# Pairs of convolution projections by seven half-size products, and attention operands ordered by residue modulo 4

## The chip, the cores and the metric

The program runs on 1 core of one Trainium2 chip. The metric is device microseconds (us) of one execution. Before the change three timed runs gave 2191.52, 2192.58 and 2193.35 us: the median is 2192.58 us.

## The reference

One inference step of a four-layer decoder for a prompt of 512 tokens and a sample group of 8 tokens, 520 columns in all, in float32. The layers are an mLSTM, a gated short convolution, a dilated attention and a pooling layer. In outline, for the two that matter here:

```python
def shortconv_mixer(h, w_in, conv_w, w_out, buf):      # w_in 1024 x 8192
    bg, cg, xb, z = jnp.split(h @ w_in, 4, axis=-1)
    cx = cg * xb
    cpad = concatenate([buf, cx], axis=1)
    y = conv_w[0] * cpad[:, 0:T] + conv_w[1] * cpad[:, 1:1+T] + conv_w[2] * cpad[:, 2:2+T]
    return (bg * y * silu(z)) @ w_out, cpad[:, -2:]

def dilated_mixer(h, w_in, w_out, pos, caches):        # three groups, dilation 1, 4, 16
    parts = jnp.split(h @ w_in, 10, axis=-1)           # q, k, v of each group, and z
    for each group: q, k = rope(q), rope(k); softmax(q k^T) over keys at that dilation; times v
    return (merge of the three groups * silu(z)) @ w_out, new keys and values
```

In the groups of dilation 4 and 16 a query sees only keys whose position has the same residue modulo 4, so their prompt attention is four blocks of 128 by 128 for each head.

## The kernel before

All activations lie transposed: a tile has 128 features on the partitions and 520 token columns. A layer is a sequence of projections. One projection (`proj`, L213) makes one output tile of 128 features: it takes eight 128 by 128 slices of one weight tile of 128 x 1024 and multiplies each by an activation tile. Float32 accuracy comes from two parts: a weight is split into `wh` and `wl` (`cast`, L169: ACT rounds at L175, DVE subtracts at L177), an activation into `hi` and `lo`, and `mm6` (L193) issues three products, hi with wh, lo with wh and hi with wl, for each of two column halves of 256 and 264: 48 matmuls a projection. The sums stand in PSUM tiles `ps` (two of them, used in turn) and are read out by DVE or ACT.

Weights are fetched by SP (L165) into three `wf` buffers and split into four pairs of `wh` and `wl`. The order of all weight tiles is the table that `plan` (L39) writes; every call of `weights` (L181) issues the split of the tile three ahead and the fetches of two more. All other work of a layer sits in generators that `tick` advances after every second `mm6`, so that ACT, DVE and POOL work stands between the matmuls in program order; each engine then runs its own instructions in that order.

The convolution layer (`conv`, from L782) makes 16 blocks of four projections: xb, cg, bg and z. A block multiplies xb and cg (L799), forms the three taps (L807 to L813), multiplies by bg (L814) and hands z to `gated`, which multiplies and splits the result (L525 to L530) for the output projection with `w_bo`. Its first blocks read activations that are not yet normalised and are scaled on the way out of PSUM.

The attention layer (`attention`, from L822) makes, for each of 8 heads, nine projections (q, k, v of three groups); `scaled` (L266) reads each out of PSUM in token order. POOL and DVE apply the rotary embedding to 32 of the 128 partitions (L875 to L880). In `attn_head` the groups 1 and 2 take every fourth column, `t[:, r:NP:4]`, as operands of the score matmuls (L925) and of the transposes of v (L936). L622 and L697 are the score matmuls and the transposes of the mLSTM layer, on columns that lie side by side.

Of the kernel before, what the change touches and what calls it, by code (L numbers as in the profile page):

```python
# [14 lines left out]
P = 128  # L15
# [13 lines left out]
DILS = (1, 4, 16)  # L29
NROWS = (128, 128, 64)  # L30
# [7 lines left out]

def plan():  # L39

    out = []

    def end(i, name, halves, begun=False):
        cs = range(2 if halves else 1)
        out.extend((name, j, c) if halves else (name, j) for c in cs for j in range(2) if c or not begun)
        out.extend((name, j, c) if halves else (name, j) for j in range(2, KD) for c in cs)
        for j in range(KD):
            if j % 4 == 0:
                out.append(("w_pe", i, j // 4))
            out.append(("w_pg", i, j))  # L50

    for hd in range(H):
        out.extend(("w_a", j) for j in (hd, 8 + hd, 16 + 2 * hd, 17 + 2 * hd, 32 + 2 * hd, 33 + 2 * hd))
    out.extend(("w_a", 48 + j) for j in range(16))
    end(0, "w_ao", True)
    for j in range(16):
        out.extend(("w_b", 16 * q + j) for q in (2, 1, 0, 3))
    end(1, "w_bo", True)
    for hd in range(H):
        out.extend(("w_c", 8 * q + hd) for q in range(9))  # L60
    out.extend(("w_c", 72 + j) for j in range(H))
    end(2, "w_co", False)
    for g in range(4):
        for n, (u, i) in enumerate(POOLED):
            if g and n == 2:
                out.extend(("w_grp", g - 1, i) for i in range(2))
            out.append(("w_d", 16 * u + 4 * g + i))
    out.extend(("w_do", j, 0) for j in range(2))
    out.extend(("w_grp", 3, i) for i in range(2))
    end(3, "w_do", True, True)  # L70
    return out

# [41 lines left out]
class Net:  # L114
    def __init__(self, ctx, tc, d):
# [5 lines left out]
        self.wp = pool("w", bufs=3)  # L121
# [7 lines left out]
        self.gate, self.finish = Gate(0.5), None  # L129
        self.wkeys, self.wf, self.wc = plan(), {}, {}  # L130
        self.wpos = self.ndma = self.ncast = 0
# [28 lines left out]

    def fetch(self, upto):
        while self.ndma < min(upto, len(self.wkeys)):
            key = self.wkeys[self.ndma]
            wf = self.wp.tile([P, 1024], F32, tag="wf", name=self.nm("wf"))
            self.nc.sync.dma_start(wf, self.d[key[0]][key[1:]])  # L165
            self.wf[self.ndma] = wf
            self.ndma += 1

    def cast(self, upto):  # L169
        nc = self.nc  # L170
        while self.ncast < min(upto, len(self.wkeys)):
            self.fetch(self.ncast + 1)
            wf = self.wf.pop(self.ncast)
            wh = self.wp.tile([P, 1024], F32R, tag="wh", name=self.nm("wh"), bufs=4)
            nc.scalar.activation(wh, wf, AF.Copy)  # L175
            wl = self.wp.tile([P, 1024], F32R, tag="wl", name=self.nm("wl"), bufs=4)
            nc.vector.tensor_sub(wl, wf, wh.bitcast(F32))  # L177
            self.wc[self.ncast] = (wh, wl)
            self.ncast += 1

    def weights(self, *key, ahead=4):  # L181
        i = self.wpos
        assert self.wkeys[i] == key, (self.wkeys[i], key)
        self.wpos += 1
        self.cast(i + ahead)
        self.fetch(i + 2 + ahead)
        return self.wc.pop(i)
# [5 lines left out]
    def mm6(self, ps, w, c, a, start, stop, m=P):  # L193
# [8 lines left out]
        for j in range(2):  # L202
            mm(out[j], wl, a[0][:, PARTS[j]], start=False, stop=stop)  # L203

# [8 lines left out]
    def proj(self, name, *idx, a):  # L213
# [5 lines left out]
        for c in range(0, n, 8):  # L219
            w = self.weights(name, *idx, *([c // 8] if n > 8 else []))  # L220
            for k in range(8):
                self.mm6(ps, w, k * P, a[c + k], c + k == 0, c + k == n - 1)
                if k % 2:
                    self.tick()
        return ps[:, BASE : BASE + T]

    def proj_pair(self, name, a, n):

        ps = self.psum(), self.psum()
        for c in range(0, n, 8):  # L230
            w = []
            for lo, hi in ((0, 7), (7, 8)) if c + 8 == n else ((0, 8),):
                for j in range(2):
                    if not lo:
                        w.append(self.weights(name, j, *([c // 8] if n > 8 else []), ahead=4 - j))
# [7 lines left out]
    def need(self, a, i):  # L243

        while len(a) <= i:
# [38 lines left out]

    def ready(self, ps):
# [14 lines left out]
    def finish_norm(self, hs, g0, wait, idle, pace):  # L300
# [6 lines left out]
        def work():  # L307
# [14 lines left out]
            for _ in range(idle):  # L322
                yield
            new = []
# [18 lines left out]


# [994 lines left out]
```

## Time and profile before

| | |
|---|---|
| median of the three timed runs | 2192.58 us |
| the profiled execution | 2191.75 us, span 2190.0 us |
| busy: PE | 2170.4 us, 99% of the span |
| DVE | 1336.6 us, 61% |
| ACT | 784.0 us, 36% |
| POOL | 226.8 us, 10% |
| DMA | 275.17 MB, mean 126 GB/s |

PE is TensorE's matmuls, PEld its weight loads, DVE VectorE, ACT ScalarE, POOL GpSimd, SP the engine that issues the transfers. A row of a group of instructions names the source line, the engine, the operation, the output and inputs (buffer numbers left out), the shapes and the count, then the busy time, the mean duration in ns and the idle time before them.

### The profile page before, as it was taken

How to read it: one execution, taken by the hardware profiler on the slowest of the kernel's cores; microseconds unless marked ns; L12 is line 12 of the kernel's file. 1: busy time of each engine (PE TensorE's matmuls, PEld its weight loads, DVE VectorE, ACT ScalarE, POOL GpSimd, SP SyncE). 2: the span in 40 equal slices, each digit the busy share in tenths (PEclk: the TensorE clock that was granted, in tenths of full speed). 3: DMA queues.
4: the chain of work that ended last, by engine and by line, in shares of the span. 5: the costliest groups of instructions: out<-in, count | busy, mean ns of one | idle time of the engine just before them, and what ended most of it. 6: DMA issues, size and time to landing. Idle time of an engine off the chain costs nothing.

```text
span 2190.0 us, 42581 instructions
## 1 busy us (share of the span) xinstructions
PE 2170.4 (99%) x17788; PEld 2154.2 (98%) x17788; DVE 1336.6 (61%) x2984; ACT 784.0 (36%) x1286; POOL 226.8 (10%) x338
## 2 busy tenths in 40 slices
PE   9999999999999999999999999999999999999998
PEld 8999999999999999999999999999999999999998
DVE  7677676653575344333467877787777466676434
ACT  6444444432442222222333323333335343222233
POOL 1101110100000000000014232232220000000000
PEclk9999999999999999999999999999999999999999
DMA  4643544333232322233233645554545233323421
GB/s 151 203 163 139 184 168 150 98 97 97 90 97 87 97 89 95 92 105 95 83 103 127 187 168 179 172 181 155 184 161 194 87 106 97 97 88 97 124 88 51
DMA packets 104643, 275.17 MB, mean 126 GB/s; under 512 B 33316, under 2 KB 37668, under 8 KB 102404
## 3 DMA queue, kind: packets, MB, share of 16 engines
q1 hardware_dynamic: 104308, 272.41, 38.3%
q8 instruction: 139, 2.28, 0.4%
q14 instruction: 52, 0.43, 0.1%
q10 hardware_dynamic: 144, 0.06, 0.0%
HBM read 249.61 MB, written 22.82 MB: 124 GB/s over the span
## 4 chain that ended last, share of the span: by engine, by line
PE 91%; DVE 3%; ACT 1%; POOL 1%; issue 0%; DMA 0%; SPq 0%; POOLq 0%; DVEq 0%; ACTq 0%
PE ps L199 27%; PE ps L201 27%; PE ps L203 27%; PE ax L925 1%; PE ax L998 1%; PE ax L201 1%; PE ax L203 1%; PE ax L199 1%; PE ax L969 1%; PE ax L654 1%; PE ax L673 1%; DVE wl L177 1%; DVE a L329 0%; POOL a L877 0%; PE ax L936 0%
## 5 line engine op out<-in xcount | busy, mean ns | idle before, releaser
L199 PE MATMUL ps<-hi,wh 128*128 128x256 f32 (+1 forms) x5280 | 1086.3, 287 | 2.1 <-DVE a L278 1.6
L201 PE MATMUL ps<-lo,wh 128*128 128x256 f32 (+1 forms) x5280 | 1062.9, 283 | 0.1
L203 PE MATMUL ps<-hi,wl 128*128 128x256 f32 (+1 forms) x5280 | 1063.1, 283 | 0.0
L199 PEld LDWEIGHTS ps<-hi,wh 128*128 128x128 f32 x5280 | 822.3, 189 | 7.6 <-issue 2.5
L201 PEld LDWEIGHTS ps<-lo,wh 128*128 128x128 f32 x5280 | 819.3, 188 | 0.3 <-DVE lo L530 0.3
L203 PEld LDWEIGHTS ps<-hi,wl 128*128 128x128 f32 x5280 | 818.3, 188 | 0.0
L177 DVE TENSOR_TENSOR wl<-wf,wh 128x1024 fp32r<-128x1024 f32 x344 | 429.2, 1249 | 397.1 <-ACT wh L175 395.5
L175 ACT ACTIVATE wh<-wf 128x1024 fp32r<-128x1024 f32 x344 | 361.0, 1051 | 253.2 <-issue 201.7
L271 ACT ACTIVATE a<-ps 128x520 f32<-128x520 f32 x94 | 56.3, 599 | 247.7 <-PE ps L203 243.5
L876 POOL TENSOR_TENSOR a<-a,a 32x520 f32<-32x520 f32 x48 | 74.0, 1542 | 386.2 <-DVE a L278 199.6
L359 DVE TENSOR_TENSOR x<-ps,x 128x520 f32<-128x520 f32 x32 | 22.4, 699 | 103.4 <-PE ps L203 103.3
L278 DVE TENSOR_TENSOR a<-ps,a 128x520 f32<-128x520 f32 x95 | 65.9, 694 | 25.9 <-PE ps L203 22.5
L282 ACT ACTIVATE a<-a 128x520 f32<-128x520 f32 x43 | 27.5, 639 | 150.2 <-DVE a L278 150.0
L259 ACT ACTIVATE hi<-x 128x520 fp32r<-128x520 f32 x32 | 20.5, 639 | 164.6 <-DVE x L359 164.6
L877 POOL TENSOR_TENSOR a<-a,a 32x520 f32<-32x520 f32 x48 | 66.4, 1384 | 124.8 <-DVE a L875 88.7
L902 ACT ACTIVATE S<-S,nmx 128x128 f32<-128x128 f32 (+1 forms) x96 | 40.0, 417 | 76.1 <-DVE nmx L899 76.1
L252 DVE CUSTOM_DVE_ANT_0 kc<-kc,qb 128x128 f32<-128x128 f32 (+1 forms) x192 | 56.8, 350 | 12.5 <-DMA kc<-kc 12.5
L252 DVE CUSTOM_DVE_ANT_0 vc<-vc,pb 128x128 f32<-128x128 f32 (+1 forms) x192 | 61.6, 379 | 0.0
L880 DVE TENSOR_TENSOR a<-a,a 32x520 f32<-32x520 f32 x48 | 37.2, 776 | 17.3 <-POOL a L877 17.3
L260 DVE TENSOR_TENSOR lo<-a,hi 128x520 fp32r<-128x520 f32 x40 | 28.0, 699 | 31.3 <-ACT hi L259 31.3
L732 DVE SCALAR_TENSOR_TENSOR Ci<-kqb,wv,Ci 128x128 f32<-128x128 f32 x128 | 37.1, 346 | 12.2 <-DMA kqb<-scr_kq 10.1
L528 ACT ACTIVATE hi<-a 128x520 fp32r<-128x520 f32 x40 | 25.4, 635 | 50.6 <-DVE a L525 50.6
(272 smaller groups left out, 1759.7 us busy)
## 6 DMA issues: line engine op xcount, KB each, us to landing
wf<-w_c SPq DMA_DIRECT2D x80, 512.0 KB
wf<-w_a SPq DMA_DIRECT2D x64, 512.0 KB
wf<-w_b SPq DMA_DIRECT2D x64, 512.0 KB
wf<-w_pg SPq DMA_DIRECT2D x32, 512.0 KB
wf<-w_d SPq DMA_DIRECT2D x32, 512.0 KB
pb<-scr_p SPq DMA_DIRECT2D x8, 1292.0 KB
Ci<-C_in SPq DMA_DIRECT2D x16, 512.0 KB
kqb<-scr_kq SPq DMA_DIRECT2D x8, 1024.0 KB
```

Of the source, the lines that this page charges most:

```text
L175: nc.scalar.activation(wh, wf, AF.Copy)
L177: nc.vector.tensor_sub(wl, wf, wh.bitcast(F32))
L199: mm(out[j], wh, a[0][:, PARTS[j]], start=start, stop=False)
L201: mm(out[j], wh, a[1][:, PARTS[j]], start=False, stop=False)
L203: mm(out[j], wl, a[0][:, PARTS[j]], start=False, stop=stop)
L252: self.nc.vector.tensor_tensor_reduce(junk, a, b, 1.0, 0.0, ALU.mult, ALU.add, out)
L271: nc.scalar.activation(dst[:, :T], ps, func, scale=scale)
L278: nc.vector.tensor_mul(dst[:, :T], ps, self.r)
L876: nc.gpsimd.tensor_mul(b[:32], t[:32], cs[0])
L877: nc.gpsimd.tensor_mul(a[:32], a[:32], cs[1])
L880: nc.vector.tensor_add(t[:32], a[:32], b[:32])
L902: nc.scalar.activation(blk, blk, AF.Exp, bias=nmx[:, i : i + 1], scale=SCALE, accum_out=l[:, i : i + 1])
```

## The change

Two parts. **Convolution:** of the 16 blocks the first three stay as they were (`NPLAIN`). In the 13 others the projections xb and cg are made together by `seven`; in the even ones of these (six blocks) bg and z too, in the odd ones (seven blocks) these two stay single. That is 19 pairs. `seven` splits a pair into a 2 x 2 scheme: two weight tiles, two halves of the 1024 inputs (four slices each) and two halves of 260 columns, and makes the four quarter results from seven products instead of eight. A product is 4 slices x 3 parts = 12 matmuls of 260 columns. The sums of weights that this needs are formed on POOL (`sum`), then split like weights into half-size tiles `hs` and `ls`; the sums of activations are formed once, after the norm, in `summed`, and kept. The quarter results are put together on ACT and DVE. The last product of a pair is issued in the middle of what follows (`flush`). The outputs of the convolution are split for `w_bo` only behind the last block, and the first half of the output projection of features 0 and 1 runs slice by slice beside that (`look`). For the single tiles of `w_b` and all of `w_bo`, and for the first tile of a pair, the low part is no longer a DVE subtraction: ACT writes minus wh, and a transfer issued by POOL adds the weight from memory to it (L258 to L260). All weights have a table of times (`due`), by which fetches, splits and sums are placed in program order; `wf` has four buffers.

**Attention:** q, k and v of groups 1 and 2 are written out of PSUM in order of residues, so that the 130 columns of a residue (128 prompt, 2 sample) lie side by side; a second pair of rotary tables in that order is loaded; the host puts the keys and values back in order.

```diff
+RES = T // 4
...
+NPLAIN = 3
+HALF = T // 2
+FBUFS, HBUFS, SBUFS = 4, 4, 4
+MOVED = ("w_b", "w_bo")
...
+def paired(j):
+
+    return 0 if j < NPLAIN else 2 - j % 2
...
+            one = at(max(ld, ld2, t - 12.8), i, "sum")
+            h1 = at(max(ld, take("wh", t + 5.76), t - 14.4), i, "high")
...
+        def low(k, tag, n=1024, pool=None):
+            t["l" + k] = new(tag, n, pool)
+            if k == "1" and it.moved:
+                nc.scalar.activation(t["l1"], f(t["h1"]), AF.Copy, scale=-1.0)
+                key = it.keys[0]
+                nc.gpsimd.dma_start(t["l1"], self.d[key[0]][key[1:]], accum_op=ALU.add)
+                return
+            nc.vector.tensor_sub(t["l" + k], t["w" + k], f(t["h" + k]))
...
+            nc.gpsimd.tensor_add(s1, w2[:, a], w2[:, b])
+            sub(w2[:, a], w1[:, a], w2[:, a])
+            sub(s2, s1, w1[:, a])
+            sub(s4, w1[:, b], s2)
...
+    def seven(self, keys, B, dst, done):
...
+        def product(out, w, name, start):
+            for k in range(4):
+                c = slice(k * P, (k + 1) * P)
+                hi, lo = B[name][k]
...
+                mm(out, w[0][:, c], hi, start=start and k == 0, stop=False, **go)
+                mm(out, w[0][:, c], lo, start=False, stop=False, **go)
+                mm(out, w[1][:, c], hi, start=False, stop=k == 3, **go)
...
+        def last():
+            product(r5, part("s4"), "22", False)
+            add(dst[0][:, HALF:], r5, u2)
+            done()
+            step()
+
+        product(r1, part("1", a), "11", True)
+        nc.scalar.activation(s1, r1, AF.Copy)
+        step()
+        product(r6, part("s2"), "T2", True)
+        add(u2, r6, s1)
+        step()
+        product(r5, part("s1"), "T1", True)
+        step()
+        product(r1, part("1", b), "21", False)
+        nc.scalar.activation(dst[0][:, :HALF], r1, AF.Copy)
+        step()
+        self.flush()
+        product(r6, part("2", a), "T3", False)
+        add(u3, r6, s1)
+        step()
+        product(r4, part("2", b), "T4", True)
+        pair = lambda x, n: x.rearrange("p (u c) -> p u c", u=2)[:, :, :n]
+        add(pair(dst[1], HALF), pair(v, HALF), u3.unsqueeze(1).broadcast_to([P, 2, HALF]))
+        step()
+        self.pend = last
...
+    def by_residue(self, ps):
...
+        t = self.act()
+        split = lambda x: x.rearrange("p (t r) -> p t r", r=4)
+        dst = t.rearrange("p (r t) -> p t r", r=4)
...
+            nc.vector.tensor_mul(dst, split(ps), split(self.r))
+        else:
+            nc.scalar.activation(dst, split(ps), AF.Copy)
...
-        rs = lambda t, r: t[:, r:NP:4]
+        rs = lambda t, r: t[:, r * RES : r * RES + P]
```

POOL in the convolution, one even and one odd block before (`cv_p` and `cv_s` collect the last rows for the output states):

```order
L803 COPY cv_p<-a_8986 128x2
L804 COPY cv_s<-a_8986 128x8
L803 COPY cv_p<-a_9226 128x2
L804 COPY cv_s<-a_9226 128x8
```

and a stretch of a block after the change (`a`, sums of weights; `wl`, a low part that a transfer completes):

```order
L260 DMA wl_8863<-w_b 128x1024
L277 TENSOR_TENSOR a_8881<-wf_8756 128x512
L278 TENSOR_TENSOR wf_8756<-wf_8710,wf_8756 128x512
L279 TENSOR_TENSOR a_8882<-a_8881,wf_8710 128x512
L280 TENSOR_TENSOR a_8883<-wf_8710,a_8882 128x512
L1067 COPY cv_p<-a_8776 128x2
L1068 COPY cv_s<-a_8776 128x8
```

Beside the two small copies, POOL now has four additions over 128 x 512 a pair and one accumulating transfer for every single tile and every pair.

DVE in the convolution, one block before, from its product of xb and cg:

```order
L799 TENSOR_TENSOR a_8986<-ps_8930,a_8928 128x520
L177 TENSOR_TENSOR wl_8995<-wf_8874,wh_8993 128x1024
L810 SCALAR_TENSOR_TENSOR a_8990<-a_8986,cols,a_8990 128x511
L811 SCALAR_TENSOR_TENSOR a_8990<-a_8986,cols,a_8990 128x510
L812 SCALAR_TENSOR_TENSOR a_8990<-cv_in,cols,a_8990 128x8
L813 SCALAR_TENSOR_TENSOR a_8990<-cv_in,cols,a_8990 128x8
L814 TENSOR_TENSOR a_8990<-ps_8992,a_8990 128x520
L177 TENSOR_TENSOR wl_9055<-wf_8935,wh_9053 128x1024
```

and half a pair after it (`ls`, low parts of the sums; `ax` and `ps`, products in PSUM):

```order
L262 TENSOR_TENSOR wl_8837<-wf_8552,wh_8822 128x1024
L1083 TENSOR_TENSOR a_8503<-a_8662,a_8503 128x520
L389 TENSOR_TENSOR a_8783<-ax_8780,a_8782 128x260
L262 TENSOR_TENSOR ls_8859<-a_8744,hs_8841 128x512
L393 TENSOR_TENSOR a_8776<-ps_8781,a_8783 128x520
L262 TENSOR_TENSOR ls_8879<-a_8743,hs_8861 128x512
L262 TENSOR_TENSOR ls_8892<-a_8745,hs_8890 128x512
L380 TENSOR_TENSOR a_8897<-ax_8895,a_8897 128x260
```

One full low part a pair is left on DVE, three half-size ones are new, and four readings of PSUM stand between them.

## Rows read from the trace of the kernel before

**Rows 1.** The page: span, and busy time of each engine.

```profile
span 2190.0 us, 42581 instructions
PE   2170.4 (99%) x17788; PEld 2154.2 (98%) x17788; DVE 1336.6 (61%) x2984; ACT 784.0 (36%) x1286; POOL 226.8 (10%) x338
```

**Rows 2.** The page: the chain that ended last, shares by engine.

```profile
PE 91%; DVE 3%; ACT 1%; POOL 1%; issue 0%; DMA 0%; SPq 0%; POOLq 0%; DVEq 0%; ACTq 0%
```

**Rows 3.** Busy time by stretch (convolution, attention): engines, granted clock, DMA share, GB/s.

```profile
610.00:980.00 370.00, 370.00 (x3089) 370.00 (x3089) 172.04 (x224) 108.58 (x134) 4.97 (x32) 1.00 0.31 95
1110.00:1700.00 590.00, 588.24 (x4760) 581.86 (x4759) 449.24 (x1366) 202.14 (x423) 160.41 (x177) 1.00 0.50 166
```

**Rows 4.** PE in order of time (start, duration): score matmuls on every fourth column.

```profile
1246.90 2.12 PE L925 MATMUL ax<-a,a 128*128 128x128 f32 x8
1248.68 0.59 PE L199 MATMUL ps<-hi,wh 128*128 128x256 f32 x2
1249.10 0.40 PE L201 MATMUL ps<-lo,wh 128*128 128x256 f32 x2
```

**Rows 5.** PE in order of time: score matmuls of the mLSTM, columns side by side.

```profile
67.83 1.05 PE L622 MATMUL ax<-a,a 128*128 128x128 f32 x8
68.64 0.49 PE L199 MATMUL ps<-hi,wh 128*128 128x256 f32 x2
68.96 0.40 PE L201 MATMUL ps<-lo,wh 128*128 128x256 f32 x2
```

**Rows 6.** Groups by line: score matmuls, and transposes of v and of the mLSTM.

```profile
L925 PE MATMUL ax<-a,a 128*128 128x128 f32 x128 | 33.8, 422 | 0.0
L936 PE MATMUL ax<-ident,a 128*128 128x128 f32 x96 | 15.2, 281 | 0.0
L697 PE MATMUL ax<-ident,num 128*128 128x128 f32 x64 | 8.3, 273 | 2.0 <-ACT Ci L728 2.0
```

**Rows 7.** Groups by line, 610 to 980 us, then of the whole span: DVE.

```profile
L177 DVE TENSOR_TENSOR wl<-wf,wh 128x1024 fp32r<-128x1024 f32 x65 | 79.6, 1225 | 153.9 <-ACT wh L175 153.9
L811 DVE SCALAR_TENSOR_TENSOR a<-a,cols,a 128x510 f32<-128x510 f32 x16 | 12.0, 750 | 0.6
L530 DVE TENSOR_TENSOR lo<-a,hi 128x520 fp32r<-128x520 f32 x16 | 11.1, 694 | 0.7 <-ACT hi L528 0.7
L799 DVE TENSOR_TENSOR a<-ps,a 128x520 f32<-128x520 f32 x13 | 9.1, 700 | 30.4 <-PE ps L203 30.4
L812 DVE SCALAR_TENSOR_TENSOR a<-cv_in,cols,a 128x8 f32<-128x8 f32 x16 | 3.5, 221 | 0.0
...
L380 DVE TENSOR_TENSOR a<-ax,a 128x264 f32<-128x264 f32 x31 | 13.1, 423 | 0.0
```

**Rows 8.** Groups by line, 610 to 980 us, then of the whole span: ACT.

```profile
L175 ACT ACTIVATE wh<-wf 128x1024 fp32r<-128x1024 f32 x65 | 68.3, 1050 | 42.2 <-issue 40.7 <-PE ps L201 1.4
L528 ACT ACTIVATE hi<-a 128x520 fp32r<-128x520 f32 x16 | 10.2, 640 | 30.7 <-DVE a L525 30.7
...
L677 ACT ACTIVATE a<-ax 128x256 f32<-128x256 f32 x32 | 12.3, 384 | 62.5 <-DVE num L676 62.4
```

**Rows 9.** Groups by line, whole span: a two-operand POOL instruction and a small copy.

```profile
L628 POOL TENSOR_TENSOR a<-a,a 128x512 f32<-128x512 f32 x8 | 10.4, 1304 | 18.4 <-DMA a<-scr_g 18.1 <-POOL os_all L500 0.3
L804 POOL COPY cv_s<-a 128x8 f32<-128x8 f32 x16 | 3.0, 190 | 0.0
```

**Rows 10.** DVE and POOL in order of time, where they meet, in the attention layer.

```profile
1137.61 1.20 DVE L177 TENSOR_TENSOR wl<-wf,wh 128x1024 fp32r<-128x1024 f32 x1
...
1137.83 2.23 POOL L876 TENSOR_TENSOR a<-a,a 32x520 f32<-32x520 f32 x1 [1.48 <-DVE a L278]
...
1230.31 1.31 POOL L876 TENSOR_TENSOR a<-a,a 32x520 f32<-32x520 f32 x1 [7.18 <-ACT a L271]
...
1231.21 1.50 DVE L177 TENSOR_TENSOR wl<-wf,wh 128x1024 fp32r<-128x1024 f32 x1 [2.34 <-ACT wh L175]
```

**Rows 11.** Weight transfers of the convolution: time SP takes to issue one (min, median, max).

```profile
L165 SPq DMA_DIRECT2D wf<-w_b x64: 327/328/328, 574.0 to 934.5; - x64
```

More of the change, by code (lines that the diff above doesn't have):

```diff
@@ L128, in __init__ @@
         self.streams = []
-        self.gate, self.finish = Gate(0.5), None
-        self.wkeys, self.wf, self.wc = plan(), {}, {}
-        self.wpos = self.ndma = self.ncast = 0
+        self.gate, self.finish, self.look = Gate(0.5), None, 0
+        self.items = plan()
+        self.ops, self.begun, self.made = due(self.items), 0, set()
+        self.wt, self.wpos, self.clock, self.pend = {}, 0, 0.0, None
         self.cols = self.cp.tile([P, NCOL], F32, name="cols")
@@ new lines, in pump @@
+    def pump(self, step=0.0):
+        nxt = self.items[min(self.wpos, len(self.items) - 1)].begin
+        self.clock = max(self.clock, min(self.clock + step, nxt))
+        by = self.clock - 0.01 if step else self.clock + 0.01
+        while self.begun < len(self.ops) and self.ops[self.begun][0] <= by:
+            self.make(*self.ops[self.begun][2:])
+            self.begun += 1
+    def fetch(self, upto):
+        for i in range(upto):
+            self.make(i, "load")
+    def cast(self, upto):
+        for i in range(upto):
+            self.make(i, "load")
+            self.make(i, "split")
@@ L182, in weights, with item @@
+    def item(self, *keys):
         i = self.wpos
-        assert self.wkeys[i] == key, (self.wkeys[i], key)
+        assert self.items[i].keys == keys, (self.items[i].keys, keys)
         self.wpos += 1
-        self.cast(i + ahead)
-        self.fetch(i + 2 + ahead)
-        return self.wc.pop(i)
+        self.clock = self.items[i].begin
+        self.pump()
+        while any((j, op) not in self.made for _, _, j, op in self.ops[self.begun :] if j == i):
+            self.make(*self.ops[self.begun][2:])
+            self.begun += 1
+        return self.wt.pop(i)
@@ L323, in work @@
                 yield
+            if sums is not None:
+                hs[:] = yield from self.summed(g0, r, sums)
+                self.hraw = False
+                return
             new = []
@@ new lines, in parts @@
+            def parts(n):
+                hi = self.act(F32R, "hi", ex if n > 3 else None)
+                nc.scalar.activation(hi, yf[n], AF.Copy)
+                yield
+                lo = self.act(F32R, "lo")
+                nc.vector.tensor_sub(lo, yf[n], hi.bitcast(F32))
+                y.append((hi, lo))
+            for j in range(NPLAIN, 16):
+                block(j)
+            self.flush()
+            self.gate.drain()
+            while self.gate.run:
+                self.gate.step()
@@ L817, in conv @@
+            self.gate.gens.extend(parts(n) for n in range(4, 16))
+            self.look = 4
             nc.sync.dma_start(d["o_conv_p"], po)
```

319 lines of the change are left out of this document (257 added, 62 removed).

## The prediction

> **What bounds the kernel now.** Begin with the busy times. PE is busy for 99% of the span, DVE for 61%, ACT for 36% and POOL for 10% [rows 1]. A busy share alone can deceive, since matmuls overlap in the trace; so take the chain that ended last: 91% of it is PE, 3% DVE and nothing is DMA [rows 2]. Then the two stretches that the change touches. In the convolution PE is busy for 370.00 of 370.00 us, at the full granted clock (1.00, the level of 2.4 GHz), with 3089 matmuls: 370.00 / 3089 = 0.1198 us each. In the attention layer PE is busy for 588.24 of 590 us [rows 3]. So every matmul that goes, or gets shorter, comes off the end, as long as the other engines keep feeding PE: DVE is busy for 172.04 of the 370 us and POOL for 4.97, but in the attention layer DVE already for 449.24 of 590.
>
> **Part 1, the pairs.** A pair was 2 projections x 48 = 96 matmuls and is now 7 products x 12 = 84, of 260 columns, the mean of 256 and 264. There are 6 x 2 + 7 x 1 = 19 pairs, so 19 x 12 = 228 matmuls go, which is also what the order of PE's instructions has less. Gain: 228 x 0.1198 = **27.3 us**.
>
> What the scheme adds, for an even block (two pairs, 168 matmuls, 20.1 us of PE), with durations of [rows 7 to 9]. On DVE: two full low parts of 1.225, six half-size low parts of about 0.69 (the row of 520 columns), six readings of a quarter result from PSUM of 0.42, two readings of 520 columns of 0.70; and as before the block's own work: three multiplications of 0.70, two long taps of 0.75, two short ones of 0.22. Sum: 2.45 + 4.14 + 2.52 + 1.40 + 2.10 + 1.50 + 0.44 = 14.6 us. On POOL: eight additions of 1.30 and two copies of 0.19, 10.8 us, and two issues of transfers. On ACT: six full roundings or negations of 1.05, six half-size ones of 0.64, four small readings of 0.38, and two passes of 0.64 for the block: 13.0 us. Each engine alone stays under 20.1, so I take these additions at nothing; the cover is PE's own time, and where it goes the next one late is DVE. An odd block has 84 + 96 = 180 matmuls, 21.6 us, against 9.3 us of DVE and 5.6 us of POOL.
>
> New waits. A low part of a sum waits on DVE for ACT, and ACT waits for POOL's sums; behind them on these queues stand the readings of PSUM, and a reading of PSUM must be done within two products (2 x 12 x 0.1198 = 2.9 us), when PE writes to the same place again. The table places the sums 12.8 us ahead of their pair. POOL's issue of an accumulating transfer waits for ACT's negation, with the next sums queued behind it; the issue itself has no row, and I put it between SP's 0.33 us and the 1.30 of one addition, so at most 2.6 us for the two of an even block, and POOL stays at 13.4 of 20.1. SP's own fetches keep their price of 0.33 us [rows 11], with one more buffer to run ahead in, and are hidden as now.
>
> POOL and DVE get in each other's way, and that is the doubtful term. At 1230.31 POOL ran a two-operand instruction for 1.31 us, and the DVE subtraction of two SBUF tiles that began inside it took 1.50 us instead of 1.225; at 1137.83 POOL began inside such a subtraction and took 2.23 us [rows 7, 10]. It looks as if only one of the two runs at a time. DVE's instructions with both inputs in SBUF make 10.6 of the 14.6 us (all but the eight readings of PSUM, 3.9 us), and with POOL's 10.8 that is 21.4 us in the 20.1 us of an even block: 1.3 us too much, six times. In an odd block it is 6.6 + 5.6 = 12.2 of 21.6, so what is left over can be made up. Bounds: 0, and 31 us (all of DVE and POOL one after the other: 14.6 + 10.8 - 20.1 = 5.3, six times). I take 2 us, near the lower end, since the odd blocks have 9 us of room.
>
> The accumulating transfers (61: 26 single tiles of w_b, 16 of w_bo, 19 pairs) have no row at all. A plain tile of 512 KB costs 0.31 x 370 / 65 = 1.76 us of all sixteen DMA engines [rows 3, 7]. Lower bound for an accumulating one: the same. Upper bound: I allow three times that, 5.3 us, for reading memory, reading the tile and writing it back. A single tile has 48 x 0.1198 = 5.75 us, so the bounds are 1.76 + 1.76 = 3.5 and 1.76 + 5.3 = 7.0 us. I take the middle of the two, two plain tiles, 5.3 us with the fetch, which is hidden; the negations on ACT (1.05 each) hide under 5.75 too. The Trainium skill (Collectives: The Full Stack, "The bandwidth ceiling") holds that a transfer that adds is slower for its second source read, not for the addition; by that rule the sum is as I have it. No run here shows it.
>
> At the end of the layer the outputs are split later than now: one rounding (0.64) and one subtraction (0.69) for each step of 12 matmuls (1.44 us), so it keeps up; at the start of the hand-over at most one such pair, 1.3 us, shows. I take 0.5.
>
> **Part 2, the residues.** The eight records of one set of score matmuls (L925) last from 1246.90 to 1248.68, and the matmul after the next starts at 1249.10: 2.20 us [rows 4]. The same on columns side by side (L622) takes 67.83 to 68.96: 1.13 us [rows 5]. There are 128 / 8 = 16 sets [rows 6]: 16 x 1.07 = **17.1 us**. The mean durations say the same less exactly. The transposes of v lose their step too, but now take 281 ns against 273 for the plain ones [rows 6]: 64 x 8 ns, 0.5 us, which I leave out. Writing out of PSUM with a step of 130 columns has no row; bounds are the 0.70 us of an eviction now [rows 7] and twice that, by the ratio 2.20 / 1.13 of PE. Each of the 48 has a whole projection, 5.75 us, before its buffer is wanted, so either way it is off the path; only in the first head, where DVE does it and is full, I allow 1 us. The loads of two more tables are small and early.
>
> **Sum.** 2191.75 (the profiled execution; 0.8 under the median, and 1.75 over its span) - 27.3 - 17.1 + 2 + 0.5 + 1 = 2150.9, and on the scale of the median 2151.7. Forecast: **2151 us**.
>
> **Rivals.**
> A. The shared path of DVE and POOL decides. For it: the two rows above, and 21.4 us in 20.1. Against: the odd blocks in between, and sums placed 12.8 us ahead. At its bound it costs 31 instead of 2 us: 2180; I see it between 2163 and 2180. The Trainium skill (SBUF — State Buffer, "Who interferes with whom") states the rule behind it: a VectorE instruction with two SBUF inputs and a GpSimd instruction that reads SBUF exclude each other for the whole instruction. By that rule the 21.4 us are hard and some of A must show; the trace agrees, with 2.23 for 1.31 us.
> B. Slower: the accumulating transfers become the bound where tiles are single. The place is the 42 single tiles, most of all the 16 of w_bo in a row. It decides as soon as one takes over 5.75 - 1.76 = 4.0 us of the sixteen engines. At 5.3 us each tile is 1.3 us late, 42 x 1.3 = 54 us: 2151 + 54 = 2205. For it: nothing in the trace shows such a transfer, and none is issued by POOL now. Against: DMA is busy for only 0.31 of the convolution.
> C. The attention gains nothing, because what PE saves comes back as late evictions by DVE, which is busy for 76% there: 2151 + 17 = 2168.
> D. The change does not do what it says: the half-size products take longer than their share. Against: 228 fewer matmuls in the order, with the same weight load before each. I give it little; it would end near 2178.
>
> **How the numbers follow.** Forecast 0.66 (2143 to 2163), A 0.16, C and D together 0.06, B 0.09, and 0.03 for a cancellation near 2192. The range must leave out at most 0.2: from 2141 (no losses, and a little more from the transposes) to 2181 it takes in the forecast, A, C and D, 0.88. A measurement of this kernel can tell about 0.2%, 4.4 us, from no change: faster is under 2188, which all but B and the cancellation are: 0.88; same 0.03; slower 0.09.
>
> **What would show it.** Right: the convolution and its output projection shorter by 27 us with PE still busy throughout; L925's successor at 275 to 300 ns instead of 422, and the attention stretch 17 us shorter. A would show as PE waiting for DVE or ACT on `ax` and `ps` in the even blocks, with POOL's additions well over 1.3 us. B would show as PE waiting for a transfer into `wl`, and a DMA share near 1 in the output projection. The forecast is wrong if PE idles over 10 us between the end of the first layer's embedding and the end of the convolution's output projection, or if the score matmuls stay over 400 ns without their step.

## The result and the profile after

The change takes 2174.74 us (median of four runs, 2174.19 to 2175.10) against 2192.05 us before (2191.13 to 2193.35, four runs beside it): ratio 0.992, 95% interval 0.9906 to 0.9934. It is faster by 17.3 us, 0.8%, which is clear of the noise. The forecast was 2151 us, 41 us faster: the time lies inside the range (2141 to 2181), but well under half of the gain came.

The page of the profile after (span 2172.4 us), its first line and its chain of waits, answering to [rows 1, 2]:

```profile
PE 2134.1 (98%) x17560; PEld 2112.8 (97%) x17560; DVE 1393.8 (64%) x3060; ACT 901.0 (41%) x1438; POOL 415.1 (19%) x491
...
PE 80%; DVE 9%; issue 3%; ACT 3%; DMA 3%; POOL 1%; SPq 0%; DVEq 0%; ACTq 0%; POOLq 0%
```

PE has the 228 matmuls less, but its share of the chain fell from 91 to 80%, and DVE's rose from 3 to 9%. A stage view tells where. Each layer opens with the same matmul of its norm, here that of the convolution, on PE's timeline:

```profile
610.40 0.82 PE L533 MATMUL ax<-a,onesd 128*128 128x256 f32 x3
```

The layers begin so at 25.48, 610.40, 1115.04 and 1780.83 us after (25.85, 608.36, 1127.43 and 1798.87 before), and the last ends with a matmul on `onesd` at 2154.47 (2171.86). The differences:

| us | first layer | convolution | attention | pooling |
|---|---|---|---|---|
| before | 582.5 | 519.1 | 671.4 | 373.0 |
| after | 584.9 | 504.6 | 665.8 | 373.6 |
| gain forecast | 0 | 27.3 - 2.5 | 17.1 - 1 | 0 |
| gain measured | -2.4 | 14.4 | 5.7 | -0.7 |

PE's waits after, in the convolution (605 to 1112 us) and then in the attention (1115 to 1782 us); the numbers are us in total, how often, and the longest:

```profile
PE ps L334 <- DVE a L485: 4.1, 3, 1.4
PE ax L364 <- DVE ls L262: 3.2, 6, 0.6
PE ps L338 <- DMA wl<-w_bo: 0.4, 1, 0.4
PE ps L334 <- ACT hi L1133: 0.2, 1, 0.2
PE ps L336 <- DVE lo L1136: 0.2, 1, 0.2
```

```profile
PE ps L334 <- DVE a L485: 3.0, 1, 3.0
PE ps L334 <- ACT a L478: 2.5, 2, 2.2
PE ax L1390 <- POOL qs L1347: 1.8, 1, 1.8
PE ax L1300 <- DVE S L1292: 1.7, 3, 0.6
PE ps L336 <- DVE lo L800: 0.8, 1, 0.8
PE ps L334 <- DVE a L500: 0.5, 1, 0.5
```

That is 8.1 us of waits in the convolution (0.2 before) and 10.3 in the attention (1.6 before). Nearly all name DVE, or an engine that had waited for DVE. What PE itself had to save came in full. One set of score matmuls, on PE's timeline:

```profile
1237.76 0.41 PE L338 MATMUL ps<-hi,wl 128*128 128x256 f32 x2
1238.00 1.05 PE L1256 MATMUL ax<-a,a 128*128 128x128 f32 x8
1238.81 0.49 PE L334 MATMUL ps<-hi,wh 128*128 128x256 f32 x2
1239.14 0.40 PE L336 MATMUL ps<-lo,wh 128*128 128x256 f32 x2
```

From the set's start to the matmul after the next it is 1.14 us, as on plain columns [rows 5], where it was 2.20 [rows 4]: 16 x 1.06 = 17.0 us.

### The profile page after: what moved, and what is told of

Read it like the earlier page. It is cut to its first block, busy times and chain, and to the rows that moved or that the text cites. A ratio compares the mean times of both kernels' runs of the same rounds, so it can differ in the third digit from the quotient of the medians.

```text
span 2172.4 us, 42676 instructions
## 1 busy us (share of the span) xinstructions
PE 2134.1 (98%) x17560; PEld 2112.8 (97%) x17560; DVE 1393.8 (64%) x3060; ACT 901.0 (41%) x1438; POOL 415.1 (19%) x491
## 4 chain that ended last, share of the span: by engine, by line
PE 80%; DVE 9%; issue 3%; ACT 3%; DMA 3%; POOL 1%; SPq 0%; DVEq 0%; ACTq 0%; POOLq 0%
PE ps L334 21%; PE ps L336 21%; PE ps L338 21%; PE ax L364 1%; DVE wl L262 1%; PE ax L362 1%; PE ax L363 1%; PE ax L334 1%; PE ax L338 1%; PE ax L336 1%; PE ps L362 1%; PE ps L363 1%; PE ps L364 1%; PE ax L1329 1%; DMA kc<-kc 1%
## 5 line engine op out<-in xcount | busy, mean ns | idle before, releaser
L334 PE MATMUL ps<-hi,wh 128*128 128x256 f32 x4672 | 964.0, 288 | 11.1 <-DVE a L485 7.1
L336 PE MATMUL ps<-lo,wh 128*128 128x256 f32 x4672 | 941.7, 283 | 1.0 <-DVE lo L800 0.8
L338 PE MATMUL ps<-hi,wl 128*128 128x256 f32 x4672 | 941.5, 283 | 0.6 <-DMA wl<-w_bo 0.4
L334 PEld LDWEIGHTS ps<-hi,wh 128*128 128x128 f32 x4672 | 727.2, 189 | 17.7 <-issue 7.4
L336 PEld LDWEIGHTS ps<-lo,wh 128*128 128x128 f32 x4672 | 725.9, 189 | 1.4 <-DVE lo L800 1.0
L338 PEld LDWEIGHTS ps<-hi,wl 128*128 128x128 f32 x4672 | 725.5, 189 | 1.0 <-DMA wl<-w_bo 0.6
L262 DVE TENSOR_TENSOR wl<-wf,wh 128x1024 fp32r<-128x1024 f32 x283 | 356.6, 1263 | 179.0 <-ACT wh L253 176.5
L502 ACT ACTIVATE a<-ps 128x520 f32<-128x520 f32 x42 | 47.6, 1133 | 133.4 <-PE ps L338 112.2
L260 POOL DMA_DIRECT2D wl<-w_b x45 | 39.8, 884 | 327.4 <-ACT wl L258 308.1
L485 DVE TENSOR_TENSOR a<-ps,a 128x520 f32<-128x520 f32 x85 | 59.0, 694 | 21.2 <-PE ps L338 17.8
L459 DVE CUSTOM_DVE_ANT_0 kc<-kc,qb 128x128 f32<-128x128 f32 (+1 forms) x192 | 58.0, 356 | 20.7 <-DMA kc<-kc 20.7
L258 ACT ACTIVATE wl<-wh 128x1024 fp32r<-128x1024 f32 x61 | 64.6, 1058 | 1.6
L262 DVE TENSOR_TENSOR ls<-a,hs 128x512 fp32r<-128x512 f32 x57 | 62.6, 1128 | 0.0
```

The source lines that it names most:

```text
L258: nc.scalar.activation(t["l1"], f(t["h1"]), AF.Copy, scale=-1.0)
L262: nc.vector.tensor_sub(t["l" + k], t["w" + k], f(t["h" + k]))
L334: mm(out[j], wh, a[0][:, PARTS[j]], start=start, stop=False)
L336: mm(out[j], wh, a[1][:, PARTS[j]], start=False, stop=False)
L459: self.nc.vector.tensor_tensor_reduce(junk, a, b, 1.0, 0.0, ALU.mult, ALU.add, out)
L485: nc.vector.tensor_mul(dst[:, :T], ps, self.r)
```

## The experiments

Seventeen kernels ran, each beside the kernel before; one of them, after_again, is the changed kernel once more. The first layer, which hardly any edit touches, came out between 584.7 and 595.7 us in kernels with the new weight table, so whole times hide effects of a few us; the stage durations, taken as above from each run's one profile, decide. They have a spread of their own: the convolution of the changed kernel is 504.4 to 504.9 us in seven of these profiles, but the attention of the changed kernel is 660.9 to 665.8 us in nine profiles whose edits do not touch it. So two single profiles can differ by 5 us in the attention without an edit to it. The third column is the 95% interval of the ratio to the kernel before.

| kernel | median us | ratio, 95% | first | conv. | attention |
|---|---|---|---|---|---|
| conv_only | 2185.61 | 0.9962 to 0.9982 | 592.8 | 504.9 | 673.6 |
| attn_only | 2184.86 | 0.9952 to 0.9978 | 584.7 | 519.1 | 661.2 |
| dots_later | 2197.77 | 1.0013 to 1.0032 | 589.1 | 504.4 | 681.6 |
| s2_earlier | 2180.63 | 0.9934 to 0.9958 | 588.4 | 512.6 | 661.5 |
| after_again | 2173.06 | 0.9910 to 0.9937 | 585.1 | 504.5 | 663.0 |
| keys_first | 2187.39 | 0.9965 to 0.9987 | 587.3 | 504.4 | 671.9 |
| v_token | 2177.42 | 0.9913 to 0.9938 | 585.2 | 504.7 | 664.1 |
| none_moved | 2201.25 | 1.0029 to 1.0054 | 585.5 | 531.5 | 664.0 |
| samp_first | 2167.88 | 0.9875 to 0.9904 | 586.2 | 504.4 | 659.2 |
| plain_unmoved | 2174.15 | 0.9897 to 0.9929 | 587.6 | 502.6 | 660.9 |
| xsums_dve | 2171.94 | 0.9895 to 0.9923 | 586.1 | 501.1 | 663.0 |
| wsums_loaded | 2168.90 | 0.9881 to 0.9909 | 584.7 | 501.7 | 663.2 |
| wsums_two_dve | 2170.22 | 0.9886 to 0.9916 | 589.9 | 501.7 | 662.9 |
| four_fixes | 2166.94 | 0.9876 to 0.9903 | 586.7 | 504.1 | 657.0 |
| before_samp_first | 2193.14 | 1.0000 to 1.0017 | 583.2 | 519.1 | 672.9 |
| best_four | 2162.35 | 0.9857 to 0.9892 | 595.7 | 498.6 | 657.1 |
| three_buffers | 2173.88 | 0.9915 to 0.9942 | 585.4 | 504.2 | 664.2 |

**The parts alone.** conv_only undoes the attention's edits in the kernel after; attn_only puts them alone into the kernel before.

> The changed kernel with the attention part undone (q, k and v in token order, one pair of rotary tables used, operands at every fourth column). Theory 1, each part loses by stalls of its own: the stretches of the two profiles give +1.8 us in the first layer, -15.0 in the convolution with its out-projection and about +1 behind it, so about 2192 - 12 = 2180 us. Theory 2, the new placing of all weight fetches (four buffers, table of times) is what disturbs the attention: then the attention is longer here than before by several us, and the time is 2185 us or more.

> The kernel before with the attention part of the change alone. Score matmuls start 120 instead of 228 ns apart, 128 x 0.108 = 13.8 us. Theory 1, the strided evictions and the waits for cached keys eat the rest: the attention is 5 to 7 us shorter, 2185 to 2187 us. Theory 2, the fetches of the changed convolution kernel's table are to blame: here the attention gains 12 to 14 us, 2178 to 2180 us.

The convolution gains 14.2 us alone and 14.4 with the other part; the attention gains 10.2 us alone, on the old weight table. So the losses are in the main each part's own. Not wholly: in conv_only the attention, with its old operands, took 673.6 us, 2.1 more than before, and attn_only's 661.2 is at the lower end of what the changed kernel gives; the new weight table may cost the attention some 2 us, and no run follows this up. In the attention neither theory fits well: 10.2 lies between them, and the changed kernel once more gave 663.0 instead of 665.8. What is lost there differs from run to run, as transfers that land at other times would make it; part of this difference is the granted clock (last section).

> The changed kernel as it is, once more, as the measure for the runs beside it. The convolution (from its first norm matmul to that of the next layer) 504.6 us again, since 504.4 to 504.9 came out in two more kernels with the same convolution. If the attention is disturbed by transfers that land at other times in every run, it comes out anywhere between 661 and 666 us; if by fixed work, 665.8 again. Time 2174 to 2181 us.

**Attention: late keys or dear evictions.**

```diff
-                    v.append(out(self.proj("w_c", 24 * g + 16 + hd, a=h)))      # v_token
+                    v.append(self.scaled(self.proj("w_c", 24 * g + 16 + hd, a=h)))
...
-        yield from wait(6)                                                      # dots_later
+        yield from wait(8)
         yield from sum_k(0)
...
-        load_k(0)                                                               # keys_first
-        load_k(1)
+        load_q(0)
+        load_q(1)
```

(dots_later also takes a step off each of two later waits; in keys_first the loads of the keys stand at the generator's start, ahead of the query's transfer.)

> The changed kernel with v written in token order again (16 fewer strided evictions, the transposes of v at every fourth column as before). Theory, transfers of keys: the attention as in the run of the changed kernel beside it, within 2 us (0.5 us for the transposes). Rival, the strided evictions of 1.13 us make ACT late: 16 x 0.53 = 8.5 us less on ACT, and the attention 3 us shorter or more.

> The changed kernel with the dot products of a sample query with the cached keys two steps later in program order (wait 8 instead of 6, the two steps taken off two later waits). Theory, DVE stands waiting for the cached keys (20.7 us in the attention, before 12.5), and behind it the maxima, ACT's exponentials and so the evictions that PE waits for: the stalls at 1186, 1324, 1385, 1390, 1515 and 1517 us, 8.9 us in all, go, or most of them: 2166 to 2170 us. Rival, the strided evictions of 1.13 us on ACT make PE wait: 2174 to 2175 us as now.

> The changed kernel with the cached keys of a sample issued by SP ahead of the transfer that carries the query to memory, not behind it. Theory, DVE waits for these keys (20.7 us), since they are issued behind a wait for the query's landing (2.9 us in head 3): the keys land 2 to 3 us earlier, and the attention is 4 to 6 us shorter than in the run of the changed kernel beside it. Rival 1, the sixteen DMA engines are full then and the queries' copies come just as late: no more than 1 us. Rival 2, the strided evictions on ACT are the cause: 0.

The evictions by residue did become dear. Groups by line in the attention of the kernel after, by residue (L502) and in token order (L478), busy us and mean ns:

```profile
L502 ACT ACTIVATE a<-ps 128x520 f32<-128x520 f32 x42 | 47.6, 1133 | 133.4 <-PE ps L338 112.2 <-issue 21.3
...
L478 ACT ACTIVATE a<-ps 128x520 f32<-128x520 f32 x27 | 15.8, 585 | 7.9 <-PE ps L338 7.9
```

But 16 of the 48 less changed nothing (664.1 against 663.0). The other two edits missed in an instructive way. dots_later only moved the wait: PE now stood at its transposes of `sT`, 13.7 us in five waits, and the attention took 681.6; its granted clock fell with these waits, to 0.98 in the mean of the stage from 1.00 in after_again. keys_first made the queries' copies late instead, and cost 9 us. DVE's wait for these copies follows the stage: after, after_again and keys_first, from DVE's waits in the attention:

```profile
DVE kc L459 <- DMA kc<-kc: 20.7, 5, 5.4
```

```profile
DVE kc L459 <- DMA kc<-kc: 17.4, 5, 4.2
```

```profile
DVE kc L459 <- DMA qb<-scr_q: 27.1, 5, 6.3
```

In the order after_again, after, keys_first this is 17.4, 20.7 and 27.1 us of waiting, with an attention of 663.0, 665.8 and 671.9. The nine profiles with the same attention say the same: the lowest waits, 16.3 to 17.0 us, stand beside 660.9 to 663.0, the highest, 20.7, beside 665.8. Why the copies are late stands on SP's queue in head 3 of the kernel after:

```profile
1367.95 0.38 SPq L1251 DMA_DIRECT2D scr_st<-st  x1
1372.09 0.33 SPq L1252 DMA_DIRECT2D st<-scr_st  x1
1372.53 0.34 SPq L1393 DMA_DIRECT2D scr_q<-qt  x1
1375.81 0.33 SPq L1364 DMA_DIRECT2D qb<-scr_q  x1
1376.19 0.42 SPq L1366 DMA_DIRECT2D kc<-kc  x1
```

The query tile `qt` was written from 1365.82 to 1366.09 us, but its transfer, issued at 1372.53, stands behind two of the softmax statistics (L1251, L1252), and SP waits for these to be made and then to come back from memory. In five of eight heads the order is this one. The one-line edit:

```diff
-        self.streams = [self.norm, rope, main, samp, self.gate]
+        self.streams = [self.norm, rope, samp, main, self.gate]
```

> The changed kernel with the sample's generator advanced ahead of the prompt's in the attention (one line), so that in every head SP issues the query's transfer ahead of the two transfers of the statistics. Now in heads 0, 2, 3, 5 and 7 it stands behind them, and SP waits there for the statistics: in head 3 the query is ready at 1366.1 and issued at 1372.5 us. Theory, this wait is what makes the copies of the query and the keys late, and DVE and then PE wait for them: the wait of DVE for kc falls from 17 to 21 us to under 6, the stalls of heads 2, 3 and 5 go and that of head 0 shrinks: the attention 5 to 8 us shorter than the 663.0 of the repeated run, 655 to 658, and the time 2165 to 2169 us. Rival, the statistics then come late and DVE waits for those: 663 or more.

> The kernel before with the sample ahead of the prompt alone. Theory, before the change the slower score matmuls covered the late keys: only the one stall of 1.9 us in the first head could go, so the attention takes 669 to 672 us instead of 671.4, and the time 2190 to 2192 us. Rival, the late keys cost as much there: 665 us or less.

SP's queue in the same head of samp_first:

```profile
1364.05 0.32 SPq L1393 DMA_DIRECT2D scr_q<-qt  x1
1365.50 0.33 SPq L1364 DMA_DIRECT2D qb<-scr_q  x1
1365.87 0.43 SPq L1366 DMA_DIRECT2D kc<-kc  x1
...
1367.57 0.39 SPq L1251 DMA_DIRECT2D scr_st<-st  x1
```

DVE's wait for `kc` fell to 1.0 us (9.9 us of idle time now stand at `wl` behind the same transfers), the attention to 659.2, below all nine profiles without the edit, though a little above the 655 to 658 expected: in the first head PE still waits 2.8 us for the queries' copies on POOL. In the kernel before, the same line takes DVE's wait for `kc` from 12.5 us to nothing, and the attention gains nothing (672.9 against 671.4). So the late transfers were there before, but covered. The likely cover is that a head's score matmuls took PE 2.1 us longer, so that PE came that much later to what waits for DVE; the change also lengthened the evictions, and no run parts the two. The evictions alone cannot cost much: best_four (below) keeps all 48 and has an attention of 657.1, 2.8 us above the 654.3 that the shorter score matmuls allow.

**Convolution: DVE, POOL and the negations.**

```diff
-        (("2", t - 4.6, t + 2.88)                              # s2_earlier
+        (("2", t - 6.5, t + 2.88)
...
-MOVED = ("w_b", "w_bo")                                        # none_moved
+MOVED = ()
...
-        self.moved = keys[0][0] in MOVED                       # plain_unmoved
+        self.moved = keys[0][0] in MOVED and (keys[0][0] != "w_b" or keys[0][1] % 16 >= NPLAIN)
...
-        sub = nc.gpsimd.tensor_sub                             # xsums_dve, in summed
+        sub = nc.vector.tensor_sub
...
-            nc.gpsimd.tensor_add(s1, w2[:, a], w2[:, b])       # wsums_two_dve
+            nc.vector.tensor_add(s1, w2[:, a], w2[:, b])
+            nc.vector.tensor_sub(s2, s1, w1[:, a])
             sub(w2[:, a], w1[:, a], w2[:, a])
-            sub(s2, s1, w1[:, a])
```

> The changed kernel with the rounding and the subtraction of the second product's weight sum 1.9 us earlier in the table of times. Theory, it is DVE's program order: the subtraction stands behind the multiplication and taps of the block before: six waits of about 0.7 us go, 4 us, 2170 to 2171 us. Rival, DVE and POOL keep each other out for so long that the same time is lost elsewhere: 2173 to 2175 us.

> The changed kernel without accumulating transfers (MOVED empty): all low parts of weights are subtracted by DVE, ACT writes no negation and POOL issues no transfer. Theory, the negations (1.05 us each on ACT, 61 of them) delay the norm's chain, and with it the reading of the first results: the stalls at 617 and 655 us (1.66 and 1.72 us) go, but DVE has 61 x 1.23 = 75 us more, and in the even blocks 2.5 us more of 20, so the waits there grow from 0.7 to 1 us or more: convolution 502 to 508 us. Rival, the accumulating transfers have no part in the loss: then the convolution is 504 to 505 us with the stalls where they are. Rival, they are needed: DVE falls behind in the even blocks, 510 us or more.

> The changed kernel with POOL's four sums of weights for each pair left out; three quarter tiles are loaded from memory in their place, so the outputs are not those of the reference. Theory, POOL's sums and DVE's two-operand instructions exclude each other: without them the subtractions of 1.23 and 0.69 us keep these times, DVE's busy time in the convolution falls by 15 us or more, and the six waits of 0.7 us go: convolution 500 to 501 us. Rival, the order of DVE's queue and its own work are the cause: the six waits stay over 0.4 us each, 503 us or more.

> The changed kernel with two of the four sums of weights of each pair on DVE instead of POOL. Theory, DVE and POOL share one path, so that what counts is the sum of both: DVE does such a sum in 0.69 us where POOL takes 1.30, so an even block has 10.6 + 4 x 0.69 + 4 x 1.30 = 18.6 us on this path instead of 21.4, and the six waits of 0.7 us shrink to under 0.3: convolution 501 to 503 us. Rival, only DVE's own queue counts: it gets 2.8 us more in 20, and the waits grow to over 1.5 us as they did without accumulating transfers (4.6 us): 510 us or more.

How DVE looks in an even block after, just ahead of one of the six waits, then POOL, then PE:

```profile
717.54 1.17 DVE L1109 TENSOR_TENSOR a<-a,a 128x520 f32<-128x520 f32 x1
719.51 0.75 DVE L1076 SCALAR_TENSOR_TENSOR a<-a,cols,a 128x511 f32<-128x511 f32 x1 [0.80 <-ACT a L1071]
...
721.36 0.69 DVE L262 TENSOR_TENSOR ls<-a,hs 128x512 fp32r<-128x512 f32 x1
```

```profile
716.00 2.16 POOL L280 TENSOR_TENSOR a<-wf,a 128x512 f32<-128x512 f32 x1
```

```profile
721.20 0.28 PE L362 MATMUL ax<-ha,hs 128*128 128x260 f32 x1
721.31 0.28 PE L363 MATMUL ax<-la,hs 128*128 128x260 f32 x1
722.10 0.39 PE L364 MATMUL ax<-ha,ls 128*128 128x260 f32 x1 [0.51 <-DVE ls L262]
722.33 0.28 PE L362 MATMUL ax<-ha,hs 128*128 128x260 f32 x1
```

The multiplication at 717.54 takes 1.17 us instead of 0.70: it ends at 718.71, 0.55 us after POOL's sum (718.16). All behind it is late: ACT's first tap (L1071) reads its output, DVE's taps wait for that, and the subtraction that PE waits for stands behind them and begins at 721.36. From start to start PE loses 0.67 us here, since the matmul at 722.10 would have begun 0.12 us after the one before, and 0.11 more at the next. The list of waits has 0.51: it counts from the modelled end of the row before. The half-size subtractions between 660 and 960 us, of after, wsums_loaded and wsums_two_dve:

```profile
L262 DVE TENSOR_TENSOR ls<-a,hs 128x512 fp32r<-128x512 f32 x57 | 62.6, 1128 | 0.0
```

```profile
L262 DVE TENSOR_TENSOR ls<-a,hs 128x512 fp32r<-128x512 f32 x57 | 37.3, 682 | 0.6 <-ACT hs L253 0.6
```

```profile
L262 DVE TENSOR_TENSOR ls<-a,hs 128x512 fp32r<-128x512 f32 x57 | 51.5, 914 | 0.6 <-ACT hs L253 0.6
```

Without POOL's sums the same instruction takes 682 instead of 1128 ns and the six waits are gone from PE's list (convolution 501.7, a little above the 500 to 501 expected). With two of four sums moved to DVE, which then has more to do, they are gone as well (501.7 too). That speaks for the sum of both engines' work, and against DVE's queue alone, as what counts; and there DVE is the cheaper place: 0.69 us a sum where POOL took 1.41 to 1.76. The Trainium skill (SBUF — State Buffer, "Who interferes with whom") states the exclusion; these three rows agree. s2_earlier, an edit of the order alone, went the other way from its theory: the six waits became others, on ACT's readings and the other sums (3.8 + 1.4 + 1.3 us), and the stage was 8 us longer. And none_moved shows how full DVE is. PE's wait in its convolution:

```profile
PE ax L364 <- DVE ls L262: 21.8, 6, 4.4
```

Two full subtractions more in an even block (2 x 1.23 us) turn six waits of 0.5 into six of 3.6 us, and the convolution takes 531.5 us, 12 more than before the change: without the accumulating transfers the pairs are a loss. Of the 27 us more than in after_again 18.6 are these waits (21.8 against 3.2); the granted clock of the convolution fell as well, to 0.98 in the mean from 1.00. The accumulating transfers themselves took 0.88 us of POOL to issue and 6.4 us to land, against 3.6 us for a plain fetch:

```profile
L260 POOL DMA_DIRECT2D wl<-w_b x45 | 39.8, 884 | 327.4 <-ACT wl L258 308.1
...
wf<-w_b SPq DMA_DIRECT2D x64, 512.0 KB, 3.6
wl<-w_b POOLq DMA_DIRECT2D x45, 512.0 KB, 6.4
```

Another part of the loss lies at the start, where the sums of activations are made.

> The changed kernel with DVE subtractions again for the 12 single tiles of the first three blocks alone (the accumulating transfers stay for the rest). Theory, ACT's negations delay the chain of the norm there: the stalls at 617 and 655 us go, 3.2 us, and the convolution takes 501 to 502 us. Rival, DVE is the one that is short there: 12 x 1.23 = 14.7 us more of DVE in the first 70 us shifts the stalls, and the convolution takes 504 us or more (without any accumulating transfer the first three stalls were 1.4, 0.9 and 3.1 us).

> The changed kernel with the sums of activations (16 subtractions of half tiles) on DVE instead of POOL. Theory, POOL's sums block DVE while they run: a DVE subtraction took 3.39 us beside them instead of 0.70, and with the sums on DVE (16 x 0.40 = 6.4 us of its own time) the stall at 630 us goes: convolution 1.5 us shorter, 503 us. Rival, DVE is simply short of time in this stretch: its 6.4 us more make the stalls at 630 and 655 us longer, 506 us or more.

In the kernel after, the first of two subtractions on DVE (the first row holds both) lasted 3.39 us, to 627.85, 0.57 us past the end of POOL's third sum:

```profile
624.46 4.55 DVE L593 TENSOR_TENSOR lo<-a,hi 128x520 fp32r<-128x520 f32 x2 [3.36 <-ACT hi L589]
```

```profile
624.82 1.07 POOL L582 TENSOR_TENSOR a<-a 128x260 f32<-128x260 f32 x1
625.52 1.06 POOL L583 TENSOR_TENSOR a<-a,a 128x260 f32<-128x260 f32 x1
626.23 1.05 POOL L584 TENSOR_TENSOR a<-a,a 128x260 f32<-128x260 f32 x1
627.36 1.09 POOL L585 TENSOR_TENSOR a<-a,a 128x260 f32<-128x260 f32 x1
```

With these sums on DVE the waits at 630 and 655 us are gone, 3.4 us instead of the 1.5 expected. plain_unmoved gains 1.9 us: the waits at 617 and 630 us go, that at 655 shrinks from 1.4 to 1.0, and a new one of 0.6 comes at 643. ACT's queue shows why the first goes: in the kernel after, two negations of 1.06 us stand ahead of the root of the norm (L534), which begins 3.3 us after the layer's first matmul; in plain_unmoved it begins 1.1 us after it.

**Together.**

> The changed kernel with four edits together: the sample ahead of the prompt in the attention, the three copies of the sample's queries ahead of POOL's other small instructions, the sums of activations on DVE, and no accumulating transfers for the first three blocks. If the causes are apart from each other, the convolution takes 504.5 - 3.4 - 1.9 = 499 us (the wait at 655 us can only go once: up to 500.5), and the attention 659.2 less about 2 of the 3.1 us that PE waits for the queries in the first head: 657; so about 2162 us. If they take the same time from DVE (14.7 us more for the subtractions, 6.4 us for the sums), the convolution stays at 502 us or more.

> The changed kernel with the four edits that helped by themselves: the sample ahead of the prompt, the queries' copies first on POOL, the sums of activations on DVE, two of the four sums of weights on DVE. If the gains add up, the convolution takes 504.5 - 3.4 - 2.8 = 498.3 us and the attention 657 us, with 586 and 373.5 us in the other two layers and 45.7 us outside the four as in the repeated run: 2160.5 us. If both edits of the sums draw on the same slack of DVE, the convolution stays at 501 to 502 us: 2164 us.

> The changed kernel with three buffers for fetched weights, as before the change, instead of four. In the first layer DVE waits 28 us for copies through memory where it waited 10 us before, and the layer is 2.4 us longer or more. Theory, SP fetches weights further ahead and the copies stand behind these fetches: with three buffers the wait is back under 15 us and the layer at 582 to 584 us. Rival, it is the new order of the splits: 585 us or more as now. In the convolution a pair needs two of the buffers at a time: with three it is longer, 506 us or more.

four_fixes adds up in the attention (657.0), not in the convolution (504.1), as its rival said: the subtractions and the sums both take DVE's time at its start. best_four leaves the first out and takes two sums of weights in: 498.6 and 657.1 us, as expected to 0.3 us. That the attention comes out at 657 us in both, against 659.2 with the order alone, is within the spread of that stage. Its median of 2162.35 us is the best of all, 0.9874 of the time before, although its first layer took 595.7 us in the profile. That layer stays open in part. DVE waits there 28 us for copies through memory (10 before), and three buffers do not change it (585.4, waits of 30 us), so the depth of the fetches is not the cause; nor does the convolution need the fourth buffer (504.2). PE waits there for `C`, which DVE makes (L943 on L931): 1.5 us in the kernel after, nothing before, and 5.6 us in best_four, where the granted clock of the layer is 0.99 in the mean against 1.00. And attn_only, on the old table, has 584.7 as well, so some 2 us come without the new table.

## Why the prediction was right or wrong

- *228 matmuls, 27.3 us, and 17.1 us for the score matmuls*: right. The count is as forecast, and a set of score matmuls is 1.06 us shorter. Rival D is out: inside a pair a matmul of 260 columns begins 0.12 us after the one before in the median, as the single ones do.
- *"Each engine alone stays under 20.1, so I take these additions at nothing", and 2 us for the shared path*: the step that failed in the convolution. Rival A was the mechanism, and the row that it rested on [rows 7, 10] was the right one to read; its sign came, PE waiting for DVE in the even blocks beside additions of 1.41 to 1.76 us on POOL. That "what is left over can be made up" in the odd block was wrong: PE waits in the even block itself. PE's six waits are 3.2 us, and removing them gave 2.8. Still more was not in the sum at all: the sums of activations at the start are POOL and DVE work of the same kind (3.4 us), placed where DVE had no room. Best_four shows both together: 6.0 us.
- *Negations hide under 5.75 us*: no wait names them in the long run, but it was wrong at the start, where ACT also makes the norm: 1.9 us.
- *Accumulating transfers, 5.3 us with the fetch*: hidden as forecast, and rival B was wrong: PE waited 0.4 us for one of them. They land in 6.4 us against 3.6 for a plain fetch, but another engine issues them through another queue, so how much of that is the adding is not shown. *0.5 us for the hand-over* to the output projection: too little, 1.8 us from start to start of the matmuls.
- *The evictions by residue off the path*: right, though ACT took 1133 ns, toward the upper bound of twice 0.70. *1 us for the first head*: too little, 1.8 us of wait for POOL's copies alone.
- *17 us off the attention's end*: the failed step there. I took the shorter PE time as gain without asking which chain would then be exposed. Rival C named late evictions; they were late (L478 and L485, 5.5 us of PE's 10.3), but behind DVE's wait for transfers, and not for want of DVE's time. samp_first gains 3.8 us and best_four 5.9 against 663.0. Beside the 11.4 us lost there stand 8.7 us more of waits than before and some 3.4 of lower clock (last section), a term that the sum did not have.
- The sum then reads 44.4 - 12.9 (convolution) - 11.4 (attention: 671.4 - 17.1 = 654.3 against 665.8) - 2.4 (first layer) - 0.7 = 17.0, plus 0.6 outside the four layers: the spans differ by 17.6 us. The list of waits has only 8.1 of the 12.9, but from start to start of PE's matmuls all of it is found: 5.9 us in the six even blocks (in each one gap of 0.7 and three of 0.1), 4.8 in the three waits at the start, 1.8 at the hand-over and 0.4 in between. Best_four still has 3.0, 1.6, 1.7 and 0.6 of these. What makes the gaps of 0.1 us no row names; that stays open.
- That 2174.74 lies in the range, and even between the 2163 and 2180 of rival A, is partly luck: of the 24 us above the forecast the shared path is about 6, and the attention, which A does not speak of, 11.4.

## What to carry to other kernels

Do not cost DVE and POOL against the bottleneck one by one: add up their instructions with two SBUF operands, block by block, and put such work on DVE as long as the sum fits (in an even block of 20.1 us, 21.4 us made PE wait and 18.6 did not). When the bottleneck engine gets faster, list the chains of fixed length (here a query's way through memory to its copies) that its old time covered, and read the queue that issues them: a queue that stands in a wait delays all behind it (6.4 us for a query here), and a one-line change of order was worth about 4 us here and nothing before the change.

## What the runs showed of the hardware

A wait of PE can cost more than its length. Four stretches about the wait of 3.0 us in the attention's first head, and two about a wait of 2.2 us in head 3, in the columns span, PE, PEld, DVE, ACT, POOL, granted clock, DMA share and GB/s:

```profile
1183.00:1186.00 3.00, 3.00 (x27) 3.00 (x27) 1.76 (x3) 2.60 (x9) 0.00 (x0) 1.00 0.79 213
1186.00:1190.00 4.00, 0.97 (x9) 0.80 (x8) 1.74 (x10) 0.00 (x0) 0.05 (x1) 1.00 1.01 390
1190.00:1194.00 4.00, 4.00 (x21) 4.00 (x22) 4.00 (x13) 0.00 (x0) 4.00 (x2) 0.58 0.27 110
1194.00:1198.00 4.00, 4.00 (x38) 3.84 (x37) 3.76 (x22) 2.15 (x4) 0.15 (x1) 0.99 0.85 230
...
1386.00:1390.00 4.00, 1.84 (x12) 1.80 (x11) 3.79 (x32) 2.55 (x5) 0.14 (x1) 0.83 0.40 114
1390.00:1394.00 4.00, 3.49 (x25) 3.19 (x24) 3.97 (x4) 1.57 (x3) 2.25 (x1) 0.75 0.59 155
```

PE was busy for 0.97 of 4 us, and in the next 4 us the granted clock was 0.58, mostly the lower level (1.2 of 2.4 GHz): 4 x 0.42 = 1.7 us of full clock are missing, on top of the wait of 3.0. About the second wait it is 4 x 0.17 + 4 x 0.25 = 1.7 us again. Before the change the granted clock is 1.00 in all of the attention. In the repeated run the second wait is not there and the clock falls once: 1.7 of the 2.8 us between the two profiles of the changed kernel.

POOL is held up too: an instruction on 8 columns (`qks`, L1348), 0.22 us in the median, took 1.91 us, while DVE ran a reading of PSUM (1.07 us) and then a subtraction (1.19 us); it ended 0.16 us after the subtraction.
